# Weight loads one step ahead, separate buffers for step-size rows, and three feed-forward pairs begun early, in a one-core hybrid decoder layer

## The chip, the cores and the metric

The kernel runs on one core of one Trainium2 chip. The metric is device time in microseconds (us) of one launch. Three runs of the kernel before took 2627.57, 2632.49 and 2633.17 us; their median is 2632.49 us.

Engine names follow the profile: PE is TensorE's matrix multiply and PEld its weight load, DVE is VectorE, ACT is ScalarE, POOL is GpSimd, SP is SyncE, which in this kernel only issues transfers. "SPq" and "ACTq" in a row are an engine's instructions that issue transfers.

## The reference

One layer of a decoder that mixes three branches, for a prompt of 1024 tokens and a sample group of 8 tokens that use the same weights. Width D is 1024. Everything is in float32.

```
xn     = rmsnorm(x)
sc_B, sc_C, sc_x, z, xBC, dt, q, gates = split(xn @ w_in)
y_a    = (sc_B * conv3(sc_C * sc_x)) @ w_sc_out
xs,B,C = silu(conv4(xBC) + bias)                       # 32 heads x 64, 4 groups, state 128
dt     = softplus(dt + dt_bias);  a = -exp(a_log)
y_b    = group_rmsnorm((SSD(xs, dt, a, B, C) + d * xs) * silu(z)) @ w_ssm_out
k, v   = rmsnorm(mem) @ w_mem_k, rmsnorm(mem) @ w_mem_v   # 256 memory tokens
y_c    = softmax(q k^T / 16) v @ w_attn_o              # 4 heads x 256
x      = x + (sum of sigmoid(gates) * y_{a,b,c}) @ w_merge_o
x      = x + (silu(rmsnorm(x) @ w_gate) * (rmsnorm(x) @ w_up)) @ w_down
y      = rmsnorm(x)
```

The SSD of the prompt is computed in chunks of 128 tokens; the sample tokens take one step of the recurrence from given states. The memory keys and values, the convolution tails and the final states are outputs too. The feed-forward width is 2816.

## The kernel before, in words

**Layout.** Activations lie with the channel on the partitions and the tokens along the row: 1024 prompt columns and 8 sample columns, 1032 in all, so a block of 128 channels is one 128 x 1032 tile. A weight block is 1024 x 128: `wblock` gives it as eight slices of 128 x 128 in one 128 x 1024 tile. Every product of float32 numbers is done as three products of rounded halves: a value is split into `hi` (a copy on ACT into the reduced type) and `lo` (the difference, on DVE), and hi·hi, hi·lo and lo·hi are summed in PSUM.

**Helpers.** `weights` loads a block (raw, issued on SP), then splits it. Raw, hi and lo tiles have three buffers each, and `in_turn` keeps each of the three kinds in program order. `gemm` multiplies one block with all eight activation tiles and calls `tick` at `pace` places on the way. `tick` runs the next entry of the queue `pend`: so pieces of other work are laid between the matmuls of a stage. An entry None skips a place. `flush` runs the rest.

`strassen` does two weight blocks (256 output channels) with seven half products instead of eight, each 24 matmuls of 258 columns over four slices of 128 channels. The activations come as prepared forms: B11 and B21 are quarters, T1, nT2, T3 and T4 sums and differences of quarters, B22 the last quarter. The weights go with them as the block itself (A), as sums of blocks (S, T; made on DVE from the raw tiles) and as one half of a block (D). The partial results are put together from PSUM into three output parts o11, o12, o22; the fourth stays in PSUM (`pa`) for the caller. The products use PSUM tiles m0, m1, m2.

**Buffers.** Most transient tiles come from one pool `ev` with five buffers of 128 x 1036 floats (`ev_tile`), handed out in program order: a tile asked for later in the program gets a buffer only when an earlier one has been released by its last reader. From the merge on there is a pool `big` with eight buffers, and each holds a tile of the residual x2 at first.

**Order.** The program order of each engine is laid out when the kernel is built: a planner takes the calls in order and may move instructions of one engine past one another by its own estimate of costs, as far as their dependences allow. At run time each engine, and each engine's queue of transfers, works strictly in that order. SP issues nearly all loads, among them raw weights, `r<-ac_d` of the SSD stage and `gt`, `mg` of the output products, and many stores.

**Stages** (us of the profiled execution):
- to about 84: the norm of x, its transposes and splits, the small step-size product.
- 84 to 121: the first C block, z0 and z1 with `gemm`. Beside them, as ticks, run `dt_softplus`, `dt_sums`, `dt_rows` (two rows tiles acT and eaT of 32 x 1024) and `dt_sample` (four tiles exs of 8 x 1024, each transposed in eight parts into `ps_ex`). After them `mem_load` asks for the two memory tiles and computes their squares on ACT (L1006, into `junkm`) and their reciprocal roots.
- 121 to about 270: five pairs of z blocks (`z_pair`, Z2 to Z10) with four `mem_t` and sixteen `kv_block` entries as ticks, which compute the memory keys and values.
- then the xBC pairs (`xbc_pair`), with Z12 and Z14 among them.
- about 550 to 1330: the SSD in 32 chunk steps (four groups of eight chunks). The queue `pend` holds the pieces of the chunks; the main thread of products between them are the steps of `fillers` (three for each of eight short-convolution blocks, eight for q) and `gates` (24).
- to about 1785: attention and the sample states as pieces, between the output products `out_in` and `out_part` (L1350 to L1360: gate rows, weights `wo{i}{m}`, product `po`, sum `mg` through DRAM); then the last output product.
- to 1880: the merge (L1455). Two halves of 516 columns, eight output blocks each. The sum of squares is gathered while the blocks are made. `norm_half` (L1405 to L1418) turns the sum into `rf`, 1/rms in all 128 partitions: one matmul with a matrix of ones for each 258 columns, then a chain of six operations, five on DVE and one square root on ACT. The forms B11 and B21 of the first half are made during the second half of the merge, as ticks.
- 1880 to 2355: the feed-forward. First the remaining forms, L1490 to L1504, in the order T1 (with the normed quarter b12, `normed`, L1422), B22 (normed), nT2 and T3, T4; T1, nT2, T3 and T4 overwrite parts of x2 on the way. Then eleven gate pairs and eleven up pairs in turn, `hidden_pair`, each a `strassen` with outputs in `big` tiles; g0 is the first. Each pair of pairs is multiplied and stored to `h_d`.
- to the end: the down product and the final norm.

In `strassen` the product B21 comes after nT2, but for the first pair of a stage (`first`), where it comes directly after B11.

## Time and profile before

| what | value |
|---|---|
| runs shown | 2627.57, 2632.49, 2633.17 us |
| profiled execution, its own time | 2626.43 us |
| its span in the profile | 2624.5 us |
| mean granted TensorE clock | 0.978 of full |
| instructions | 42664 |
| TensorE busy | 2527.5 us |
| DVE busy | 1468.6 us |
| ACT busy | 933.1 us |
| POOL busy | 182.1 us |

The times in a profile are us from the start of the span. A row of the timeline has the start, the duration, the engine, the line of the kernel, the operation, the tile written and those read, the shapes, and in brackets how long the engine had been idle before and what released it. A row of the waits says which instruction of an engine waited for which other one, the sum of these waits, their count and the longest. A group row has the busy time and the mean of one in ns, and the idle time ahead. A row of windows has the busy time and, in brackets, the instructions of each engine in a stretch, then the mean granted clock of TensorE, the busy share of the DMA engines, and GB/s. Rows of transfers are named by the tile they fill.

### The profile page before, as it was taken

Reading aid. Unit: us, or ns where it says so; the run is one execution under the profiler, and the core shown is the slowest. Engines: PE = TensorE matmul, PEld = TensorE weight load, DVE = VectorE, ACT = ScalarE, POOL = GpSimd, SP = SyncE. Lnnn points to the kernel's source line nnn. Section 1 sums busy time; section 2 is a strip of 40 time slices with the busy share of each in tenths; the row PEclk is TensorE's granted clock in tenths of the full one; section 3 lists DMA queues with packets and bytes.
Section 4 is the critical chain, followed back from the end, with each engine's and each line's share of the span. In section 5 each row is a group of like instructions: output and inputs, shape, how many; then the busy total and the mean of one; then the engine's idle time right before and its main releaser. Section 6 shows DMA issues by size and latency. Waiting matters only on the chain.

```text
span 2624.5 us, 42664 instructions
## 1 busy us (share of the span) xinstructions
PE 2527.5 (96%) x18009; PEld 2458.8 (94%) x18009; DVE 1468.6 (56%) x2049; ACT 933.1 (36%) x1426; POOL 182.1 (7%) x203
## 2 busy tenths in 40 slices
PE   7899999999998999999999999999889999999998
PEld 6899999999998999999999997999889999999998
DVE  5744677866666655545576643344865454554316
ACT  5543444553333235254342321213343333342202
POOL 0000000013213123023000000000000000000000
PEclk8899999999999999999999999999989999999999
DMA  5244333376645556665487757844322222255211
GB/s 188 85 138 153 122 113 106 122 197 148 173 142 137 160 186 159 187 190 160 128 287 246 275 190 251 286 137 142 104 65 76 71 89 74 81 200 164 72 41 65
DMA packets 388301, 387.72 MB, mean 148 GB/s; under 512 B 15574, under 2 KB 334662, under 8 KB 388103
## 3 DMA queue, kind: packets, MB, share of 16 engines
q1 hardware_dynamic: 369534, 334.17, 42.3%
q10 hardware_dynamic: 18577, 50.84, 5.1%
q8 instruction: 141, 2.31, 0.4%
q14 instruction: 49, 0.40, 0.1%
HBM read 278.84 MB, written 106.34 MB: 147 GB/s over the span
## 4 chain that ended last, share of the span: by engine, by line
PE 70%; DMA 4%; DVE 4%; ACT 1%; issue 1%; SPq 0%; POOL 0%; ACTq 0%; DVEq 0%; POOLq 0%
PE po L167 10%; PE ps_g L167 10%; PE pd L167 8%; PE ps_scc L167 4%; PE pm L1455 4%; PE ps_scx L167 4%; PE ps_q L167 3%; PE ps_scb L167 3%; DMA kc<-in_cache_mem_k_dram 2%; PE py L730 1%; PE pss L748 1%; PE po L722 1%; PE u0m L218 1%; PE u20m L218 1%; PE g20m L218 1%; PE u18m L218 1%
## 5 line engine op out<-in xcount | busy, mean ns | idle before, releaser
L1568 DVE TENSOR_TENSOR x<-pd,x 128x1032 f32<-128x1032 f32 x24 | 29.6, 1231 | 130.8 <-PE pd L167 130.8
L675 ACT ACTIVATE r<-r,acum 128x128 f32<-128x128 f32 x256 | 78.9, 391 | 34.1 <-DMA r<-ac_d 32.7
L1355 DVE TENSOR_TENSOR gt<-po,gt 128x1032 f32<-128x1032 f32 x24 | 29.5, 1229 | 81.3 <-PE po L167 81.2
L709 POOL TENSOR_TENSOR xdd<-xdt,decst 128x512 f32<-128x512 f32 x32 | 46.5, 1455 | 272.0 <-DVE xdt L705 272.0
L534 DVE SCALAR_TENSOR_TENSOR ax<-u,prm,ax 128x1024 f32<-128x1024 f32 x44 | 56.3, 1280 | 0.0
L815 POOL TENSOR_TENSOR st<-st,xb 128x512 f32<-128x512 f32 x32 | 43.7, 1367 | 36.2 <-DVE xb L809 34.0
L702 ACT COPY bT<-bp 128x128 f32<-128x128 f32 x32 | 8.5, 265 | 105.3 <-DVE cbm L700 105.3
L739 DVE SCALAR_TENSOR_TENSOR x<-x,dpar,yt 128x128 f32<-128x128 f32 x128 | 37.5, 354 | 10.1 <-ACT yt L737 9.2
L703 DVE TENSOR_TENSOR r<-r,cbm 128x1024 f32<-128x1024 f32 x32 | 39.1, 1222 | 6.5 <-ACT r L676 5.9
L761 POOL TENSOR_TENSOR s<-s,cdec 128x512 f32<-128x512 f32 x28 | 39.1, 1396 | 44.9 <-DVE s L754 34.1
L748 PE MATMUL pss<-xdd,bT 128*128 128x512 f32 x64 | 33.7, 609 | 7.4 <-ACT bT L702 7.4
L754 DVE TENSOR_TENSOR s<-pss,s 128x512 f32<-128x512 f32 x28 | 19.2, 687 | 38.2 <-PE pss L748 38.2
L812 POOL TENSOR_TENSOR st<-st,es 128x512 f32<-128x512 f32 x32 | 36.5, 1142 | 18.7 <-DMA st<-in_state_ssm_dram 15.2
L730 PE MATMUL py<-r,xdt 128*64 128x128 f32 x512 | 35.0, 279 | 0.0
L700 DVE TENSOR_TENSOR cbm<-bp,tri 128x128 f32<-128x128 f32 x32 | 9.3, 290 | 45.7 <-PE bp L695 45.7
L676 ACT ACTIVATE r<-r 128x1024 f32<-128x1024 f32 x32 | 33.9, 1059 | 0.7
L726 DVE TENSOR_TENSOR yt<-po,ea 128x512 f32<-128x512 f32 x28 | 19.2, 686 | 25.9 <-PE po L722 25.9
L1391 DVE TENSOR_TENSOR gt<-po,gt 128x1032 f32<-128x1032 f32 x8 | 9.9, 1233 | 40.6 <-PE po L167 40.6
L1194 ACT ACTIVATE pr<-psa,mx 128x256 f32<-128x256 f32 x32 | 15.0, 472 | 48.3 <-DVE mx L1192 40.9
L1184 DVE TENSOR_TENSOR kc<-kc,qb 128x1024 f32<-128x1024 f32 x16 | 19.6, 1222 | 21.8 <-DMA kc<-in_cache_mem_k_dram 21.8
L730 PEld LDWEIGHTS py<-r,xdt 128*64 128x64 f32 x512 | 27.3, 136 | 4.2 <-issue 0.9
L821 DVE TENSOR_TENSOR xc<-bcb,st 128x512 f32<-128x512 f32 x32 | 21.9, 684 | 16.5 <-POOL st L815 15.1
(7946 smaller groups left out, 8666.9 us busy)
## 6 DMA issues: line engine op xcount, KB each, us to landing
gt<-gt_d SPq DMA_DIRECT2D x32, 516.0 KB
r<-ac_d SPq DMA_DIRECT2D x32, 512.0 KB
gt_d<-g ACTq DMA_DIRECT2D x24, 516.0 KB
mg_d<-gt SPq DMA_DIRECT2D x24, 516.0 KB
mg<-mg_d SPq DMA_DIRECT2D x24, 516.0 KB
xs_d<-ax ACTq DMA_DIRECT2D x22, 516.0 KB
hr<-h_d SPq DMA_DIRECT2D x22, 516.0 KB
zs_d<-z ACTq DMA_DIRECT2D x16, 516.0 KB
```

What stands on the lines that cost most here:

```text
L167: PE.matmul(ps[:, n, :CW], wt[:, ks], x[:, n * CW : (n + 1) * CW], start=(k == 0 and i == 0), stop=(k == nk - 1 and i == 2),)
L218: PE.matmul(ps[:, n, :HC], wt[:, ks], x[:, n * HC : (n + 1) * HC], start=(start and kt == 0 and i == 0), stop=(kt == 3 and i == 2), skip_g ...
L534: V.scalar_tensor_tensor(acc[:, :T], u[:, j : j + T], w[j], acc[:, :T], op0=ALU.mult, op1=ALU.add)
L675: S.activation(r[:, h, :], r[:, h, :], AF.Relu, scale=-1.0, bias=acum[:, c, h0 + h : h0 + h + 1])
L703: V.tensor_tensor(r, r, bc(cbm.unsqueeze(1), [P, HPG, P]), op=ALU.mult)
L709: G.tensor_tensor(b3(xdd, HPG), b3(xdt, HPG), bc(decst[:, c, hs].unsqueeze(2), [P, HPG, 64]), op=ALU.mult)
L730: PE.matmul(py[hp : hp + 64, (h // 2) * P : (h // 2 + 1) * P], xdt[:, h * 64 : (h + 1) * 64], r[:, h, :], start=True, stop=True,)
L739: V.scalar_tensor_tensor(xg[t][:, cs], xg[t][:, cs], dpar[:, g * 4 + t : g * 4 + t + 1], yt[:, t, :], op0=ALU.mult, op1=ALU.add,)
L748: PE.matmul(pss, bT, xdd, start=True, stop=True)
L761: ins = G.tensor_tensor(b3(s_new, HPG), b3(state["s"], HPG), bc(cdec[:, c, hs].unsqueeze(2), [P, HPG, 64]), op=ALU.mult,)
L815: G.tensor_tensor(st, st, xb, op=ALU.add)
L1455: PE.matmul(ps[:, n, :HC], wt[:, ks], x[:, half * HT + n * HC : half * HT + (n + 1) * HC], start=(k == 0 and i == 0), stop=(k == KD - 1 an ...
```

## The change

Six things are changed.

1. A step of the SSD stage and of the output products is now a `Step` that knows its weights. `run_next` issues the raw load of the following step's weights before it runs the current step; `weights` takes the loaded tile if there is one.
2. acT, eaT and the four exs tiles come from the pool of the step-size stage, under one tag with two buffers, no longer from `ev`. The squares of the memory tiles and their roots move from `mem_load` into an entry `mem_rms` of `pend`, behind a None; the squares are written into a tile that is filled later (`memT`), so `junkm` goes.
3. Z12 moves from between the xBC pairs to behind Z10, ahead of the `flush`. The flag `first` goes: for Z2 the product B21 stands at its usual place.
4. `norm_half` is called once for a half: six matmuls, each with 128 columns of the squares as weights, give the sums of the 516 tokens as six columns (three pieces that overlap for each 258), the chain runs on these columns, and six transposes and two ACT copies spread the result over the partitions.
5. `st_early` does the products B11 and B21 of the first gate pair, the first up pair and the second gate pair (g0, u0, g2) ahead of the remaining forms, and holds their sums in three ev tiles. It loads the first raw block of each pair for that, once more than before. These three pairs then run `strassen` with five products; three more operations on DVE and one copy on ACT put the parts together, in four output parts.
6. The remaining forms come in the order T1, nT2 (which now does the normed quarter b22), T3, B22, T4. For T3 both the difference and `lo` are on GpSimd. The weight sums of g0 stand between the forms: S after T1 (`st_sums`), T after T3 (`st_sums2`).

```diff
...
-    def weights(src, name):
+    loaded = {}
+
+    def load_raw(src, name):
         raw = wp.tile([P, 1024], F32, tag="raw", name=name + "r")
...
+        return raw
+
+    class Step:
+
+
+        def __init__(self, src, name, run):
+            self.src, self.name, self.run = src, name, run
+
+        def __call__(self):
+            self.run()
+
+    def run_next(*queues):
+
+        q = [f for d in queues for f in d]
+        (queues[0] or queues[-1]).popleft()
+        if len(q) > 1 and isinstance(q[1], Step):
+            loaded[q[1].name] = load_raw(q[1].src, q[1].name)
+        q[0]()
+
+    def weights(src, name):
+        raw = loaded.pop(name, None)
+        if raw is None:
+            raw = load_raw(src, name)
         hi = wp.tile([P, 1024], F32R, tag="whi", name=name + "h")
         lo = wp.tile([P, 1024], F32R, tag="wlo", name=name + "l")
         in_turn("hi", S.copy(hi, raw))
...
+    def st_prod(forms, ps, w, off, f, start):
+        for kt in range(4):
+            xh, xl = forms[f][kt]
+            ks = slice(off + kt * P, off + (kt + 1) * P)
+            for i, (wt, x) in enumerate(((w[0], xh), (w[0], xl), (w[1], xh))):
+                for n in range(2):
+                    PE.matmul(
+                        ps[:, n, :HC], wt[:, ks], x[:, n * HC : (n + 1) * HC],
+                        start=(start and kt == 0 and i == 0), stop=(kt == 3 and i == 2),
+                        skip_group_check=True,
+                    )
+
+    def st_early(blocks, forms):
+
+
+        held = []
+        for i, (src1, nm, o1) in enumerate(blocks):
+            wA = st_split(st_raw(src1, f"{nm}Er"), f"{nm}E")
+            ps = st_ps(f"m{i}", f"{nm}e")
+            st_prod(forms, ps, wA, 0, "B11", True)
+            S.copy(h3(o1[:, HS[1]]), hv(ps))
+            held.append((wA, ps, o1))
+        for wA, ps, o1 in held:
+            st_prod(forms, ps, wA, 512, "B21", False)
+            S.copy(h3(o1[:, HS[0]]), hv(ps))
+
+    def st_sums(src1, src2, nm, sums):
         raw1, raw2 = st_raw(src1, f"{nm}r1"), st_raw(src2, f"{nm}r2")
...
+        sa = sums(f"{nm}sa")
+        V.tensor_add(sa[:, :512], raw2[:, :512], raw2[:, 512:])
+        V.tensor_add(sa[:, 512:], sa[:, :512], raw1[:, :512])
+        return raw1, raw2, sa, st_split(sa, f"{nm}S")
+
+    def st_sums2(raw1, raw2, sa, nm, sums):
+        sb = sums(f"{nm}sb")
+        V.tensor_add(sb[:, :512], raw1[:, :512], raw2[:, :512])
+        V.scalar_tensor_tensor(
+            sb[:, 512:], sa[:, 512:], -1.0, raw1[:, 512:], op0=ALU.mult, op1=ALU.subtract
+        )
+        return st_split(sb, f"{nm}T")
+
+    def strassen(src1, src2, forms, nm, sums, outs, early=None, after_t3=None, ready=None):
+
+
+        if ready is None and early is None:
+            raw1, raw2 = st_raw(src1, f"{nm}r1"), st_raw(src2, f"{nm}r2")
         tags = ("m0", "m1", "m2") if count[0] % 2 == 0 else ("m2", "m1", "m0")
         count[0] += 1
-        pa, pb, pc = (pst[0].tile([P, 2, 512], F32, tag=t, name=f"{nm}{t}") for t in tags)
+        pa, pb = (st_ps(t, f"{nm}{t}") for t in tags[:2])
 
         def prod(ps, w, off, f, start):
...
+        o11, o12, o21, o22 = outs()
+        if early is None:
+            pc = st_ps(tags[2], f"{nm}{tags[2]}")
+            wA = st_split(raw1, f"{nm}A")
+            prod(pa, wA, 0, "B11", True)
+            S.copy(h3(o11), hv(pa))
+        tick()
+        if ready is not None:
+            raw1, raw2, sa, wS, wT = ready
+        elif early is not None:
+            raw1, raw2, sa, wS = st_sums(src1, src2, nm, sums)
+        else:
+            sa = sums(f"{nm}sa")
+            V.tensor_add(sa[:, :512], raw2[:, :512], raw2[:, 512:])
+            V.tensor_add(sa[:, 512:], sa[:, :512], raw1[:, :512])
+            wS = st_split(sa, f"{nm}S")
+        prod(pb, wS, 0, "T1", True)
+        S.copy(h3(o22), hv(pb))
+        prod(pa, wS, 512, "nT2", early is not None)
+        if early is None:
+            S.copy(h3(o12), hv(pa))
             prod(pc, wA, 512, "B21", True)
             V.tensor_tensor(h3(o11), hv(pc), h3(o11), op=ALU.add)
-
-        wA = st_split(raw1, f"{nm}A")
-        prod(pa, wA, 0, "B11", True)
-        S.copy(h3(o11), hv(pa))
+        else:
+            S.copy(o21, o12)
+            V.tensor_sub(o22, o22, o12)
+            V.tensor_tensor(h3(o12), hv(pa), h3(o12), op=ALU.add)
...
+        if ready is None:
+            wT = st_sums2(raw1, raw2, sa, nm, sums)
         prod(pa, wT, 0, "T3", False)
         if after_t3 is not None:
             after_t3()
...
     def dt_rows():
-        act_ = ev_tile("acT", (HEADS, T))
-        eat_ = ev_tile("eaT", (HEADS, T))
+        act_, eat_ = (pd_.tile([HEADS, T], F32, tag="wide", bufs=2, name=n) for n in ("acT", "eaT"))
...
         for i in range(4):
-            exs = ev_tile(f"exs{i}", (NS, 1024))
+            exs = pd_.tile([NS, 1024], F32, tag="wide", bufs=2, name=f"exs{i}")
...
         def s0():
             hold["c"] = c_()
 
+        def at(col, nm, f):
+            return Step(wblock(w_in, col + ct * P), f"w{nm}{ct}", f)
+
...
-        return [s0, s1, s2]
+        return [at(C_SCC, "scc", s0), at(C_SCX, "scx", s1), at(C_SCB, "scb", s2)]
 
...
             t = ev_tile(f"mem{m}", (P, D))
             SY.dma_start(t, a["mem_prompt"][0, m * P : (m + 1) * P, :])
             mem_sb.append(t)
-        junk = ev_tile("junkm", (P, D))
+
+    def mem_rms():
         for m in range(2):
+            junk = memT[m][0].rearrange("p k c -> p (k c)")
             S.activation(junk, mem_sb[m], AF.Square, accum_out=mst[:, m : m + 1])
         rsqrt(pm, mrs, mst, D, [P, 2], "m")
 
...
     mem_load()
+    pend.extend([None, mem_rms])
     pend.extend(lambda m=m, half=half: mem_t(m, half) for m in range(2) for half in range(2))
     pend.extend(lambda j=j, q=q: kv_block(j, q) for j in range(8) for q in range(2))
     z_step(1)
...
-    for i in (2, 4, 6, 8, 10):
+    for i in (2, 4, 6, 8, 10, 12):
         z_pair(i)
     flush()
     mem_stack.close()
...
-    z_pair(12)
     xbc_pair(4, 5)
     xbc_pair(6, 7)
     xbc_pair(8, 9)
...
     while pend:
-        (fillers or gates).popleft()()
+        run_next(fillers, gates)
...
-                lambda w=w, m=m, i=i: out_part(w, m, (0, 8, 8)[i] + m, i > 0, f"{i}{m}") for m in range(KD)
+                Step(
+                    wblock(w, m * P), f"wo{i}{m}",
+                    lambda w=w, m=m, i=i: out_part(w, m, (0, 8, 8)[i] + m, i > 0, f"{i}{m}"),
+                )
+                for m in range(KD)
             )
         while pend:
-            gates.popleft()()
+            run_next(gates)
...
-    def norm_half(half, sq, i):
-        if i == 0:
-            rfs[half] = ev_tile(f"rf{half}")
+    def norm_half(half, sq):
+        rfs[half] = ev_tile(f"rf{half}")
         t = rfs[half]
...
+        starts = [n * HC + c for n in range(2) for c in (0, P, HC - P)]
+        ps = sm_ps(f"psf{half}")
+        for i, c in enumerate(starts):
+            PE.matmul(ps[:, i : i + 1], sq[:, c : c + P], ones[:, 0:1], start=True, stop=True)
+        r, v = t[:, 600:606], t[:, 606:612]
+        s_ = t[:, 612:618]
+        V.tensor_scalar(v, ps[:, :6], 1.0 / D, EPS, op0=ALU.mult, op1=ALU.add)
+        S.activation(s_, v, AF.Sqrt)
+        V.reciprocal(r, s_)
+        V.tensor_mul(s_, r, r)
+        V.scalar_tensor_tensor(s_, v, -0.5, s_, op0=ALU.mult, op1=ALU.mult)
+        V.scalar_tensor_tensor(r, s_, 1.5, r, op0=ALU.add, op1=ALU.mult)
+        for n in range(2):
+            ps = sm_ps(f"psr{half}{n}")
+            for i in range(3):
+                c = starts[i]
+                PE.transpose(ps[:, c : c + P], bc(r[:, 3 * n + i : 3 * n + i + 1], [P, P]), ident)
+            S.copy(t[:, n * HC : (n + 1) * HC], ps[:, :HC])
 
...
         if half == 0:
-            pend.extend([None, None] + [lambda i=i, sq=sq: norm_half(0, sq, i) for i in range(2)] + [None])
+            pend.extend([None, None] + [lambda sq=sq: norm_half(0, sq)] + [None])
             for kt in range(4):
                 pend.extend([lambda kt=kt: form_first(kt), None, lambda kt=kt: form_second(kt), None])
         else:
             flush()
-            for i in range(2):
-                norm_half(1, sq, i)
+            norm_half(1, sq)
...
+    ffn = {"g": a["w_ffn_gate"][0], "u": a["w_ffn_up"][0]}
+    early = {(nm, j): ev_tile(f"{nm}{j}e") for nm, j in (("g", 0), ("u", 0), ("g", 2))}
+    st_early([(wblock(ffn[nm], j * P), f"{nm}{j}", t[:, :TT]) for (nm, j), t in early.items()], forms)
     for kt in range(4):
         b12, b11 = normed(kt, 1), x2[kt][:, HS[0]]
         V.tensor_sub(b11, b12, b11)
         form("T1", kt, b11)
+    ev_sums = lambda n: ev_tile(n, (P, 1024))
+    g0 = st_sums(wblock(ffn["g"], 0), wblock(ffn["g"], P), "g0", ev_sums)
     for kt in range(4):
-        form("B22", kt, normed(kt + 4, 1))
-    for kt in range(4):
-        t1, b12, b22 = x2[kt][:, HS[0]], x2[kt][:, HS[1]], x2[kt + 4][:, HS[1]]
+        t1, b22 = x2[kt][:, HS[0]], normed(kt + 4, 1)
         V.tensor_sub(t1, t1, b22)
         form("nT2", kt, t1)
-        V.tensor_sub(b12, b22, b12)
-        form("T3", kt, b12)
+    for kt in range(4):
+        b12, b22 = x2[kt][:, HS[1]], x2[kt + 4][:, HS[1]]
+        G.tensor_tensor(b12, b22, b12, op=ALU.subtract)
+        form("T3", kt, b12, G)
+    g0 = (*g0, st_sums2(*g0[:3], "g0", ev_sums))
+    for kt in range(4):
+        form("B22", kt, x2[kt + 4][:, HS[1]])
     for kt in range(4):
         t2, b21 = x2[kt][:, HS[0]], x2[kt + 4][:, HS[0]]
         V.scalar_tensor_tensor(t2, t2, -1.0, b21, op0=ALU.mult, op1=ALU.subtract)
         form("T4", kt, t2)
 
...
+        e = early.get((nm, j))
 
         def outs():
-            o.extend([big(f"{nm}{j}o1"), big(f"{nm}{j}o2")])
-            return o[0][:, HS[0]], o[0][:, HS[1]], o[1][:, HS[1]]
-
+            o.extend([big(f"{nm}{j}o1") if e is None else e[:, :TT], big(f"{nm}{j}o2")])
+            return tuple(t[:, c] for t in o for c in HS)
+
+        src = ffn[nm]
         pa = strassen(
             wblock(src, j * P), wblock(src, (j + 1) * P), forms, f"{nm}{j}",
-            lambda n: ev_tile(n, (P, 1024)), outs, nm == "g" and j == 0,
+            ev_sums, outs, e, ready=g0 if (nm, j) == ("g", 0) else None,
         )
-        return o[0], o[1], pa
+        return o[0], o[1], pa if e is None else h3(pa)
 
...
     st_stack.close()
```

88 lines of the change are left out of this document (26 added, 62 removed).

## The prediction

> **What bounds the kernel now.** I read the page first. Its parts one and two have the span, the busy time of each engine, and TensorE's busy tenths in 40 slices of 65.6 us.
>
> ```profile
> span 2624.5 us, 42664 instructions
> PE 2527.5 (96%) x18009; PEld 2458.8 (94%) x18009; DVE 1468.6 (56%) x2049; ACT 933.1 (36%) x1426; POOL 182.1 (7%) x203
> PE   7899999999998999999999999999889999999998
> ```
>
> TensorE bounds it: 2624.5 − 2527.5 = 97 us idle in all, and no product is removed by this change. So a gain can only come from idle time, or from matmuls that run at a lowered clock behind idle time. The tenths dip in the first two slices, at 787 to 853 us and at 1837 to 1968 us. Next I read the waits of TensorE (who waited for whom, sum, count, longest).
>
> ```profile
> PE g0m L218 <- ACT g0o L232: 13.3, 1, 13.3
> PE po L167 <- ACT wo24h L127: 7.8, 1, 7.8
> PE g0m L218 <- ACT T10h L263: 7.5, 1, 7.5
> PE pss L748 <- ACT bT L702: 7.4, 1, 7.4
> PE Z2m L218 <- ACT z L621: 5.3, 1, 5.3
> PE Z4m L218 <- ACT Z4Th L198: 2.5, 1, 2.5
> PE Z8m L218 <- ACT Z8Th L198: 2.5, 1, 2.5
> ```
>
> Each is a single event. Then I cut windows around them; the columns are microseconds, busy PE, weight loads, DVE, ACT, POOL, the granted clock, the DMA share and GB/s.
>
> ```profile
> 95.90:116.00 20.10, 17.55 (x116) 15.91 (x114) 16.39 (x26) 11.85 (x17) 0.20 (x1) 0.92 0.17 52
> 116.00:121.30 5.30, 0.02 (x1) 0.00 (x0) 1.78 (x5) 2.07 (x4) 0.00 (x0) 0.60 0.94 316
> 121.30:141.00 19.70, 19.41 (x137) 19.01 (x138) 13.38 (x29) 12.20 (x25) 0.00 (x0) 0.85 0.34 118
> 1631.30:1643.70 12.40, 2.72 (x24) 0.88 (x22) 2.49 (x3) 2.37 (x6) 0.00 (x0) 0.69 0.80 295
> 1643.70:1657.80 14.10, 14.10 (x73) 14.10 (x74) 3.65 (x3) 2.39 (x3) 0.00 (x0) 0.79 0.83 226
> 1886.40:1893.90 7.50, 0.05 (x1) 0.00 (x0) 7.50 (x13) 2.53 (x5) 0.00 (x0) 0.64 0.16 46
> 1901.50:1914.80 13.30, 0.04 (x1) 0.00 (x0) 13.30 (x23) 7.28 (x12) 0.00 (x0) 0.53 0.00 0
> 1914.80:1920.80 6.00, 5.57 (x28) 5.36 (x28) 5.99 (x10) 3.42 (x6) 0.00 (x0) 0.63 0.00 0
> 1949.30:2354.70 405.40, 405.39 (x3362) 405.18 (x3360) 203.92 (x254) 137.32 (x178) 0.00 (x0) 1.00 0.29 94
> ```
>
> The reader is to see three places of different kinds: at 116–121 us TensorE waits with a full DMA, at 1631–1644 us it waits for weights, and at 1886–1920 us DVE is busy all the time, so the feed-forward forms bound the work there. From 1949 to 2355 us TensorE is never idle: 20 pairs, 140 half products of 24 matmuls, 405.4/140 = 2.896 us each.
>
> **Part one: the exs and acT/eaT rows in their own pool, the squares of mem as a tick, z12 moved.**
>
> ```profile
> 98.38 0.59 ACT L491 ACTIVATE eaT<-ps_acT 32x512 f32<-32x512 f32 x1 [0.24 <-DVE acT L490]
> 98.88 0.99 ACT L600 COPY uC<-ps_C 128x1032 f32<-128x1032 f32 x1
> 114.97 1.03 ACT L621 ACTIVATE z<-ps_z 128x1032 f32<-128x1032 f32 x1 [2.91 <-PE ps_ex L510]
> 119.21 1.06 ACT L1006 ACTIVATE junkm<-mem 128x1024 f32<-128x1024 f32 x1 [3.20 <-DMA mem<-in_mem_prompt_dram]
> 120.26 1.01 ACT L621 ACTIVATE z<-ps_z 128x1032 f32<-128x1032 f32 x1
> ```
>
> The five ev buffers are handed out in program order. So uC, z0 and the two mem tiles can't be written until the rows ahead of them (acT, eaT, the four exs) are done with: z0's Silu runs right behind the exs chain, the mem loads start only then, the Square of mem waits for them, and z1's Silu, which Z2's first matmul waits for, stands behind that Square on ACT. With the rows in a pool of their own and the Square pended, this chain goes. Idle in the first two windows is 2.55 + 5.28 = 7.8 us; the lowered clock costs 17.55 × 0.08 = 1.4 us and 19.41 × 0.15 = 2.9 us. That is 12.1 us in all. The exs chain itself stays, now through two buffers, and the Square still runs before mem's transposes; I leave 2 us for that: −10, bounds −12.5 and +4 (the wait for mem comes back inside Z2, with as much again at half clock; mem_t and all the key and value ticks queue behind it).
>
> Two new ticks shift the key and value blocks, and z12 now runs beside them. Z4 and Z8 lose 2.5 us each where ACT copies a key block ahead of the T weights; I count one more such place: +2.5, bounds 0 and +4. Z12's own products only move, and the xbc pair that it leaves has no wait in the list above.
>
> **Part two: weights asked for one step ahead.** Of each step the raw load on SP is issued before the previous step's pieces; the cast and the subtraction stay.
>
> ```profile
> 1001.95 0.37 SPq L122 DMA_DIRECT2D wg5r<-in_w_in_dram  x1
> 1044.94 1.05 ACT L127 CAST wg5h<-wg5r 128x1024 fp32r<-128x1024 f32 x1 [1.12 <-PE ps_g L167]
> 1637.64 0.69 SPq L122 DMA_DIRECT2D wo24r<-in_w_ssm_out_dram  x1
> 1642.60 1.04 ACT L127 CAST wo24h<-wo24r 128x1024 fp32r<-128x1024 f32 x1
> ```
>
> Elsewhere a load is asked 43 us before its cast (wg5), so earlier asking buys nothing there; at wo24 it is asked 5 us ahead, behind the stores of the last attention pieces on SP. This ask now stands ahead of them. The window 1631–1644 holds 12.40 − 2.72 = 9.7 us idle, of which 7.8 for this weight; the next one runs at 0.79, 14.10 × 0.21 = 3.0 us. The small gaps of 1.9 us stay and keep some of the low clock: I take −9 (7.8 and 1.2 of the 3.0), bounds 0 and −11.
>
> The Trainium skill (TensorE: Matmul & The Clock Gate, Part 1) says that the clock falls after an idle window of about 3.4 us. By that rule the gaps of 1.9 us would not lower it, all 3.0 us would return, and the sum below would be about 2 us lower.
>
> What an early ask can cost is another matter: SP works in order, and each ask waits at its head until one of the three raw buffers is free. Behind it stand, in the SSD stage, the loads of r.
>
> ```profile
> 835.60 0.66 SPq L669 DMA_DIRECT2D r<-ac_d  x1
> 835.60 12.51 DMA r<-ac_d
> r<-ac_d SPq DMA_DIRECT2D x32, 512.0 KB
> ```
>
> This load took 12.5 us and stands in the chain that ended last, ahead of the wait for bT of 7.4 us. It can come out better (−11 with its clock) or worse by the new order of instructions. I take 0.
>
> **Part three: the feed-forward start.** Now: B11, then the norm of the second half, T1, nT2, and so on, with DVE as the bound.
>
> ```profile
> 1879.59 0.48 PE L218 MATMUL g0m<-B110h,g0Ah 128*128 128x258 f32 x2 [0.88 <-DVE x L1462]
> 1881.74 0.43 DVE L1413 TENSOR_SCALAR rf<-psf 128x258 f32<-128x258 f32 x1 [0.85 <-PE psf L1412]
> 1890.27 0.42 DVE L1418 SCALAR_TENSOR_TENSOR rf<-sq,rf 128x258 f32<-128x258 f32 x1
> 1913.69 0.62 ACT L263 CAST T40h<-x 128x516 fp32r<-128x516 f32 x1 [0.65 <-DVE x L1502]
> 1914.21 0.58 ACT L232 COPY g0o<-g0m 128x516 f32<-128x516 f32 x1
> ```
>
> The 13.3 us wait is not one for ACT: g0's output needs a `big` buffer, and that is one of x2's, which is free only once the first T4 form has been written (1913.7). g0's last product ends at 1929.0, reckoned back from the end of the last pair over the 147 half products of the other 21: 2354.7 − 147 × 2.896.
>
> After the change six half products (B11 and B21 of g0, u0, g2) come first: 17.4 us of TensorE, to about 1898, with outputs in ev buffers. They cover the T1 and part of the nT2 forms. g0, u0, g2 then have five products each. But o21 and o22 are still `big` tiles and still wait for the first T4 form. So the date is set by DVE's list up to there. The norm chain took 1881.74 to 1890.69, 8.95 us for two halves; on six columns it must be under one half, 4.5, and I take 3: rf at about 1884.8. Six matmuls and six transposes for each half, against two matmuls: +1 in all, bounds 0 and +2. Then: T1 12 operations, nT2 12, B22 4, T4 2, at 7.50/13 = 13.30/23 = 0.58 us, 17.4; g0's sums, four of half width, 2.3; and the subtractions of S, T and one E, 1.2 each.
>
> ```profile
> 812.47 1.23 DVE L128 TENSOR_TENSOR wscc7l<-wscc7r,wscc7h 128x1024 fp32r<-128x1024 f32 x1 [1.56 <-ACT wscc7h L127]
> 831.37 2.07 DVE L128 TENSOR_TENSOR wscx7l<-wscx7r,wscx7h 128x1024 fp32r<-128x1024 f32 x1
> 832.43 2.16 POOL L815 TENSOR_TENSOR st<-st,xb 128x512 f32<-128x512 f32 x1
> L815 POOL TENSOR_TENSOR st<-st,xb 128x512 f32<-128x512 f32 x32 | 43.7, 1367 | 36.2 <-DVE xb L809 34.0
> ```
>
> The first of these rows gives the 1.2. In sum 17.4 + 2.3 + 3.6 = 23.3, to 1908.1. The T3 forms move to POOL: eight operations of 1.37 us, 11 us. They aren't free, since the same subtraction took 1.23 us alone and 2.07 beside POOL work, which itself took 2.16 for 1.37: DVE lost 0.84 in 2.07 us that hold about 2.07 × 1.37/2.16 = 1.3 us of POOL work, between 0 and all of it. I take three quarters, towards the upper end, since T3 falls into the stretch in which DVE is never idle: +8.4, to 1916.5 (bounds 1908.1 and 1919.1). Behind that stand the copy of o22, two DVE operations, 3 × 0.58 = 1.7, then the products T3, B22 and T4, 8.7, and half clock at their start (28 matmuls in 5.57 us is 0.2 us each, against 0.121: 1.9 us for one product). g0 ends at 1916.5 + 12.3 = 1928.8. 143 products stay behind it instead of 147: gain 1929.0 + 4 × 2.896 − 1928.8 = 11.8, less 2 for waits that the early pairs meet (three extra E splits, 512 KB each to load, during merge): −10, bounds −18 (no contention) and −2.
>
> The Trainium skill (SBUF — State Buffer, Who interferes with whom) says that a DVE instruction with two SBUF inputs and a GpSimd instruction that reads SBUF share a port pair under an exclusive lock, the loser blocked for the whole instruction. By that rule all 11 us fall on DVE, and the gain here is about 7. The rows agree in kind: both engines lengthen.
>
> **Sum.** −10 + 2.5 − 9 − 10 + 1 = −25.5 on the profiled execution's 2626.43 us (span 2624.5 and 1.93 around it): 2600.9. The runs shown lie 1.1 to 6.7 us above that execution, the median 6.06; with 4 for that, 2605 us.
>
> **The rivals.** Two gains can fail alone. The ask at wo24 stays behind the stores, if the order of SP puts it there: 2605 + 9 = 2614. Or POOL locks DVE for the whole of T3, and T3's own forms, at 2.16 us each, 17.3 us, come later than the nT2 product: then the feed-forward start gains 2, not 10, and the time is 2613. For it speaks the DVE's full windows; against it, that TensorE has six products to do meanwhile. Larger: the wait for bT goes by chance (−11) or POOL costs DVE nothing (−8): about 2587 to 2597.
>
> Slower: early asks at the head of SP hold back the loads of r. Against it, the wait list holds just one such stall in 32 chunks, and asks are few (one a step); for it, a stall there already cost 7.4 us with a landing of 12.5. If each chunk waits 1 us more, 32 us come on top: 2637. It decides from 30.5/32, about 0.95 us in each chunk; the place to see it is r's idle time on ACT.
>
> No change: the same mechanism at about 0.8 us a chunk, which uses up the gain. About 0.2% (5.3 us) is what a measurement of this kernel can tell.
>
> **How the numbers follow.** Likeliest 0.52 (own range 2597 to 2612); one or both of the two gains failing 0.22; larger 0.10; no measurable change 0.04; slower 0.12. That gives faster 0.84, same 0.04, slower 0.12. The range runs from the larger case, 2585, to where both gains fail and part one gives little, 2628: it leaves out the slower case and the ends of the larger one.
>
> **What would show it.** Right: z1's Silu no longer behind a Square, Z2's first matmul at about 111 us; no wait of po for wo24h; the waits for g0o and T10h gone or under 5 us; g0's end minus the four products at about 1929. A third wait of 2.5 us at a Z pair. Wrong: r's waits on ACT longer in many chunks; a wait of g0m for T3 forms; DVE operations of 516 columns well over 0.75 us beside POOL; a new wait at Z2 for mem.

## The result and the profile after

The changed kernel took 2607.4 us (median of four runs, 2603.75 to 2610.7) where the kernel before took 2631.22 us on the same chip: ratio 0.9911, 95% interval 0.9893 to 0.9929. The forecast was 2605 us, faster.

The head of the page of the changed kernel:

```profile
span 2601.7 us, 42760 instructions
PE 2521.7 (97%) x18037; PEld 2453.8 (94%) x18037; DVE 1466.5 (56%) x2037; ACT 936.6 (36%) x1434; POOL 197.9 (8%) x211
```

TensorE's idle time fell from 97 to 80 us (2601.7 − 2521.7). Its busy time fell as well, by 5.8 us with 28 matmuls more, so this part is time at a lowered clock. Its waits after, the longest ones of the places concerned:

```profile
PE pss L815 <- ACT bT L769: 6.5, 1, 6.5
PE g0m L236 <- DVE nT22l L329: 4.3, 2, 3.6
PE g0m L236 <- DVE g0e L309: 3.7, 1, 3.7
PE Z4m L236 <- ACT Z4Th L223: 2.5, 1, 2.5
PE Z8m L236 <- ACT Z8Th L223: 2.5, 1, 2.5
PE Z12m L236 <- ACT Z12Th L223: 2.5, 1, 2.5
```

The waits for wo24h and T10h are gone, the one for g0o is down to 0.8 us, the wait for bT stands about as it was, and a third Z pair waits 2.5 us. Smaller waits for forms, and one for an addition (g0e), have come up at g0 in place of the two long ones.

To see where the time went, I cut both executions at the same six instructions: the first z0 product, the first product of the SSD stage, the first product with wo00, the first with wo24, the first of the feed-forward, the first of the down product. Windows of the kernel before, and then of the changed one (columns as in the prediction):

```profile
84.14:547.77 463.63, 446.80 (x3621) 442.87 (x3619) 301.09 (x419) 213.75 (x280) 6.88 (x46) 0.98 0.40 126
547.77:1334.14 786.37, 773.49 (x5148) 742.18 (x5148) 466.25 (x668) 302.59 (x512) 173.83 (x147) 0.99 0.60 167
1334.14:1643.69 309.55, 294.13 (x1904) 277.76 (x1904) 165.09 (x225) 87.72 (x171) 0.00 (x0) 0.98 0.71 245
1879.59:2355.57 475.98, 452.23 (x3700) 450.30 (x3701) 260.84 (x339) 166.81 (x220) 0.00 (x0) 0.97 0.27 87
```

```profile
79.39:540.50 461.11, 446.47 (x3620) 442.17 (x3618) 302.58 (x423) 217.26 (x283) 6.94 (x46) 0.99 0.39 127
540.50:1329.26 788.76, 772.37 (x5147) 740.79 (x5147) 465.61 (x666) 302.36 (x512) 173.98 (x147) 0.99 0.61 167
1329.26:1628.48 299.22, 291.65 (x1885) 277.14 (x1886) 163.74 (x223) 86.38 (x166) 0.00 (x0) 0.99 0.71 241
1864.84:2332.49 467.65, 454.74 (x3714) 452.76 (x3715) 261.99 (x331) 165.39 (x223) 15.65 (x8) 0.98 0.28 90
```

| stretch | before | after | difference | forecast |
|---|---|---|---|---|
| start to z0 | 84.1 | 79.4 | −4.7 | 0 |
| z and xBC pairs | 463.6 | 461.1 | −2.5 | −7.5 |
| SSD stage | 786.4 | 788.8 | +2.4 | 0 |
| wo00 to wo24 | 309.6 | 299.2 | −10.3 | −9 |
| wo24 to the feed-forward | 235.9 | 236.4 | +0.5 | 0 |
| feed-forward | 476.0 | 467.7 | −8.3 | −9 |
| down product and end | 268.9 | 269.2 | +0.3 | 0 |
| span | 2624.5 | 2601.7 | −22.8 | −25.5 |

The sum is near, but two of its terms are not: the start gained 4.7 us with no part of the change in it, and the z stage gained a third of what was forecast.

### The profile page after: what moved, and what is told of

Same layout as the page of the kernel before. It is cut to its first block, busy times and chain, and to the rows that moved or that the text cites. A ratio compares the mean times of both kernels' runs of the same rounds, so it can differ in the third digit from the quotient of the medians.

```text
span 2601.7 us, 42760 instructions
## 1 busy us (share of the span) xinstructions
PE 2521.7 (97%) x18037; PEld 2453.8 (94%) x18037; DVE 1466.5 (56%) x2037; ACT 936.6 (36%) x1434; POOL 197.9 (8%) x211
## 4 chain that ended last, share of the span: by engine, by line
PE 68%; DMA 5%; DVE 4%; issue 1%; ACT 1%; SPq 0%; POOL 0%; ACTq 0%; DVEq 0%; POOLq 0%
PE ps_g L192 10%; PE po L192 10%; PE pd L192 8%; PE ps_scc L192 4%; PE pm L1535 4%; PE ps_q L192 4%; PE ps_scx L192 3%; PE ps_scb L192 3%; DMA kc<-in_cache_mem_k_dram 1%; PE py L797 1%; PE pss L815 1%; PE po L789 1%; DMA r<-ac_d 1%; PE u20m L236 1%; PE g20m L236 1%
## 5 line engine op out<-in xcount | busy, mean ns | idle before, releaser
L742 ACT ACTIVATE r<-r,acum 128x128 f32<-128x128 f32 x256 | 78.9, 391 | 36.2 <-DMA r<-ac_d 34.8
L1424 DVE TENSOR_TENSOR gt<-po,gt 128x1032 f32<-128x1032 f32 x24 | 29.5, 1230 | 70.4 <-PE po L192 69.1
L1583 POOL TENSOR_TENSOR x<-x,x 128x516 f32<-128x516 f32 x4 | 8.9, 2235 | 635.8 <-DVE x L1502 635.8
L1542 DVE TENSOR_TENSOR x<-pm,xT 128x516 f32<-128x516 f32 x16 | 11.1, 695 | 36.2 <-PE pm L1535 36.2
```

The source lines that it names most:

```text
L742: S.activation(r[:, h, :], r[:, h, :], AF.Relu, scale=-1.0, bias=acum[:, c, h0 + h : h0 + h + 1])
```

## The experiments

Times below are compared with runs of the kernel before on the same chip, or by stretches of the profile. A stretch is that of one profiled execution. How far one order spreads can be read from the versions whose edit lies elsewhere: with the changed order the z and xBC stretch took 460.7 to 461.1 us in five executions, and the feed-forward 466.9 to 467.7 us in six; the profile above is the longest of each. In the SSD stage TensorE has the same order of instructions in all versions, and it took 784.9 to 790.2 us. Six versions ran once, five of them in 2602 to 2607 us and the one without asks in the output products in 2615; single whole times can't tell 2 or 3 us apart, so for these versions only the stretches are read.

**T3 on DVE.** Both operations of T3 go back to DVE:

```diff
-        G.tensor_tensor(b12, b22, b12, op=ALU.subtract)
-        form("T3", kt, b12, G)
+        V.tensor_sub(b12, b22, b12)
+        form("T3", kt, b12)
```

> The changed kernel with the T3 forms (difference and lo) back on DVE. Theory 1, POOL and DVE exclude each other: in the changed kernel nine DVE operations of 516 columns beside POOL took about 1.77 us each against a pitch of 0.60, 10.5 us lost, to save DVE eight operations of 0.60, 4.8 us. Then DVE's list to the first T4 form gets 5.7 us shorter, no 516-column operation of DVE is above 0.76 us, and the time falls by 3 to 7 us against the changed kernel, to about 2602. Theory 2, POOL's help pays and the late nT2 lo is only a matter of order: DVE gets eight more operations, the time rises by up to 5 us, to about 2612.

It took 2596.87 us against 2627.18 (ratio 0.9888, interval 0.9871 to 0.9904). First rows of POOL (the second is a group) and of DVE in the changed kernel, with its window of that time; then the window of equal length of this run, its feed-forward stretch, and its longest wait at g0.

```profile
1879.99 3.90 POOL L1583 TENSOR_TENSOR x<-x,x 128x516 f32<-128x516 f32 x1 [633.76 <-DVE x L1502]
L329 POOL TENSOR_TENSOR T30l<-x,T30h 128x516 fp32r<-128x516 f32 x2 | 3.4, 1736 | 0.0
1882.04 0.69 DVE L329 TENSOR_TENSOR nT20l<-x,nT20h 128x516 fp32r<-128x516 f32 x1
1882.64 2.46 DVE L1502 SCALAR_TENSOR_TENSOR x<-x,prm,rf 128x516 f32<-128x516 f32 x2
1891.44 1.77 DVE L1579 TENSOR_TENSOR x<-x,x 128x516 f32<-128x516 f32 x1
1898.18 0.68 DVE L1590 SCALAR_TENSOR_TENSOR x<-x,x 128x516 f32<-128x516 f32 x1
1882.60:1898.20 15.60, 8.25 (x60) 7.33 (x58) 15.60 (x13) 6.51 (x12) 13.04 (x8) 0.84 0.02 5
```

```profile
1884.80:1900.40 15.60, 7.75 (x64) 7.47 (x62) 15.60 (x26) 8.18 (x14) 0.00 (x0) 0.87 0.12 34
1867.02:2329.50 462.48, 451.35 (x3714) 450.53 (x3715) 258.22 (x339) 165.10 (x223) 0.00 (x0) 0.99 0.28 90
PE g0m L236 <- ACT g0o L300: 9.5, 1, 9.5
```

In 15.6 us DVE and POOL together have 13 + 8 operations, counting those that the edges of the window cut; DVE alone has 26. An operation of 516 columns that takes 0.69 alone takes 1.77 beside POOL, and POOL's take some 1.7 (its first one, ahead of the window, 3.90). The rows read as if the two engines took turns here, one operation each. The feed-forward is 5.2 us shorter with T3 on DVE (4.4 against the shortest with the changed order), where theory 1 had 3 to 7. Of the 5.2 us, 1.8 are idle time of TensorE, and 3.4 are its busy time for the same products (454.74 and 451.35), so the larger part is time at a lowered clock behind the waits. The 9.5 us wait for the buffer of x2 is then the one that shows; the smaller waits for forms are gone.

**One early pair instead of three.**

```diff
-    early = {... for nm, j in (("g", 0), ("u", 0), ("g", 2))}
+    early = {... for nm, j in (("g", 0),)}
```

> The changed kernel with early products for g0 alone, two half products instead of six. Theory 1, DVE's list of forms sets the end of g0: g0 ends as long after its first early product as now (53 us), and four half products of 2.896 us more stand behind it: plus 11.6 us on the feed-forward stage, less up to 1.5 us for two E splits that DVE is spared. Theory 2, TensorE sets the end of g0 and the early products are only moved: the stage stays within 2 us.

```profile
1861.73:2336.06 474.33, 457.18 (x3715) 454.11 (x3715) 260.65 (x328) 166.59 (x222) 14.55 (x8) 0.97 0.27 88
```

6.7 us longer, between the theories: four products later by 11.6 us would be theory 1, so by this sum g0 itself ends 4.9 us earlier. Two E splits of 1.2 us that DVE is spared are 2.4 of it; the other 2.5 I can't assign. TensorE's columns show 4.2 of the 6.7 us as idle time and 2.4 as busy time for the same products. The extra early products are worth some 7 us, not 11.6.

**The norm's chain on 258 columns.**

```diff
-        for i, c in enumerate(starts):
-            PE.matmul(ps[:, i : i + 1], sq[:, c : c + P], ones[:, 0:1], start=True, stop=True)
...
+        for i in range(2):
+            c = slice(i * HC, (i + 1) * HC)
+            ps = sm_ps(f"psf{half}{i}")
+            PE.matmul(ps[:, :HC], ones, sq[:, c], start=True, stop=True)
...
```

> The changed kernel with the norm's chain on 258 columns, as before the change. Theory 1, DVE's list sets the end of g0: the chain takes about 9 us again instead of 4.0 (from the last square sum to the first normed quarter), and the feed-forward stage gets 3 to 6 us longer. Theory 2, the early products cover it: the stage stays within 1 us.

Two rows of DVE of this run, the chain's first operation and the first normed quarter, and its feed-forward window; the last row is the first normed quarter in the changed kernel:

```profile
1866.76 0.86 DVE L1486 TENSOR_SCALAR rf<-psf 128x258 f32<-128x258 f32 x2 [0.79 <-PE psf L1485]
1873.05 1.42 DVE L1495 SCALAR_TENSOR_TENSOR x<-x,prm,rf 128x516 f32<-128x516 f32 x2
1864.09:2333.40 469.31, 454.35 (x3700) 451.53 (x3701) 267.50 (x336) 165.86 (x222) 13.27 (x8) 0.98 0.28 90
```

```profile
1870.90 1.42 DVE L1502 SCALAR_TENSOR_TENSOR x<-x,prm,rf 128x516 f32<-128x516 f32 x2 [1.37 <-ACT rf L1498]
```

The stage is 1.7 us longer (2.4 against the shortest with the changed order), less than theory 1 had and more than theory 2. Counted from the first feed-forward product, the first normed quarter comes at 8.96 us with the wide chain (1873.05 − 1864.09) and at 6.06 with the narrow one (1870.90 − 1864.84): from where the wide chain starts, 2.67 us after that product, it takes 6.3 us, and in its place the short chain with its matmuls, transposes and copies takes 3.4.

**The second tick behind T3.** A version that goes beyond the change: in `strassen`

```diff
-        tick()
         if ready is None:
             wT = st_sums2(raw1, raw2, sa, nm, sums)
         prod(pa, wT, 0, "T3", False)
+        tick()
```

> The changed kernel with the second tick of a pair moved behind the T3 product, so that the T weights are cast on ACT ahead of a key or value block's copies. Theory 1, the three waits of 2.5 us at Z4, Z8 and Z12 come only from ACT's order: all three go, the time falls by 5 to 8 us against the changed kernel, to about 2600. Theory 2, the wait only changes its place (the block's own weights must now be split between two half products 2.9 us apart): new waits of 1 to 3 us in most pairs, time the same or up to 8 us longer.

It took 2591.08 us (ratio 0.9871, interval 0.9853 to 0.9888), and all three waits are gone. The stretch of the z and xBC pairs:

```profile
79.81:529.57 449.76, 442.43 (x3621) 439.23 (x3619) 301.80 (x421) 216.72 (x283) 7.46 (x46) 1.00 0.40 130
```

11.4 us shorter: 7.5 for the waits, and 4.0 less busy time of TensorE for the same products (446.47 to 442.43), since some of the waits had lowered its clock behind them. More than theory 1 expected.

**Both edits.** 

> Both edits at once: second tick behind the T3 product, T3 forms on DVE. They lie in different stages, so theory 1 adds them: minus 11.4 us (first z product to the first product of the SSD stage, 461.1 to 449.8) and minus 5.2 us (feed-forward stage, 467.7 to 462.5) against the changed kernel; ratio to the kernel before about 0.985, some 2587 us on this chip. Theory 2, part of the gain of the tick run was its SSD stage (2.3 us shorter, by another order): then 2 to 3 us less is gained.

2584.75 us against 2625.54: ratio 0.984, interval 0.9826 to 0.9855, the best version here, faster than both kernels (the changed one has 0.9911 against the kernel before on its own chip).

```profile
1851.05:2313.68 462.63, 451.50 (x3715) 450.68 (x3715) 258.44 (x339) 165.22 (x224) 0.00 (x0) 0.99 0.28 91
80.58:530.39 449.81, 442.61 (x3621) 439.32 (x3619) 301.75 (x420) 216.61 (x283) 7.42 (x46) 1.00 0.40 130
```

The two gains add to within 0.2 us in their stretches.

**The first T4 form earlier.** As the former run, and in the order of the forms:

```diff
+    form_t4(0)
     g0 = (*g0, st_sums2(*g0[:3], "g0", ev_sums))
     for kt in range(4):
         form("B22", kt, x2[kt + 4][:, HS[1]])
-    for kt in range(4):
+    for kt in range(1, 4):
+        form_t4(kt)
```

> As the former, and the first T4 form ahead of g0's second weight sums and of B22. Theory 1, what g0 waits for (9.5 us ahead of its B22 product with T3 on DVE) is the buffer of x2 that the first T4 form releases: the wait falls by 4 to 6 us and the feed-forward stage by 2 to 4 us against the former run. Theory 2, another wait takes its place at once (the addition into g0's early part, which DVE does behind all T4 forms, holds back T3): the stage stays within 1 us.

```profile
1852.07:2315.97 463.90, 453.02 (x3714) 451.73 (x3715) 258.23 (x339) 165.29 (x223) 0.00 (x0) 0.99 0.28 91
PE g0m L236 <- ACT g0Th L223: 6.8, 1, 6.8
```

Nothing gained (2586.06 us, the stretch 1.3 us longer): the wait for the buffer is gone, which shows that it was the first T4 form that it waited for, and a wait for g0's T weights takes its place, whose sums DVE now makes later. So DVE's list as a whole looks like the bound there, not one place in it.

**Weights asked ahead in the output products alone**, in the kernel before: `run_next`, `Step` and `loaded` as in the change, used for the `out_part` steps only.

> The kernel before with one part alone: weights asked one step ahead in the output products. Theory 1, the wait of 7.8 us for wo24's weights goes by this part alone: from the first wo00 matmul to the first wo24 matmul 299 to 301 us instead of 309.6, the whole 9 to 11 us shorter. Theory 2, without the other parts the request still comes behind the stores on SP: a wait of more than 4 us stays. At the start, where this kernel has the order of the kernel before: if the 4.7 us that the changed kernel gained ahead of the first z product are chance of the clock, that product starts anywhere from 79 to 84 us; if they are the order's, at 84.

2612.04 against 2625.54 us (ratio 0.9941, interval 0.9926 to 0.9956). The wait for wo24h is gone; the stretch from wo00 to wo24:

```profile
1332.07:1630.52 298.45, 292.30 (x1885) 278.01 (x1885) 163.81 (x223) 86.32 (x166) 0.00 (x0) 0.98 0.69 242
```

11.1 us shorter than in the kernel before. This run also bears on the start. Up to the attention stage every engine has the instructions of the kernel before in the same order, and still its first z0 product starts at 79.03 us, not at 84.14. A window of 4 us of the kernel before; then, of this run, z0's first product, the same window, and the SSD stage:

```profile
52.00:56.00 4.00, 4.00 (x15) 3.17 (x16) 3.44 (x9) 2.64 (x7) 0.00 (x0) 0.52 0.22 76
```

```profile
79.03 0.48 PE L192 MATMUL ps_z<-xnh,wz0h 128*128 128x344 f32 x2
52.00:56.00 4.00, 4.00 (x24) 3.38 (x25) 3.46 (x9) 2.38 (x8) 0.00 (x0) 1.00 0.22 77
541.92:1332.07 790.15, 772.91 (x5147) 741.40 (x5148) 465.82 (x668) 302.65 (x512) 175.74 (x147) 0.99 0.60 167
```

The clock was granted at half in this window in one execution, and in full in the other. In the eleven profiles of the other versions z0 starts at 78.6 to 81.4 us. So the 4.7 us of the profiled difference are no gain of the change, but chance of that one execution, or at most of the chip that it ran on. The last row says the same of the SSD stage: 790.2 us with the instruction order that took 786.4, so the +2.4 us there is within what one order shows.

**Squares at the load.**

```diff
-    pend.extend([None, mem_rms])
+    mem_rms()
```

> The changed kernel with the squares of the memory tiles computed where they are loaded, not as a tick. Theory 1, the Square stands on ACT ahead of z1's Silu and waits for the memory tiles: Z2 starts 2 to 5 us later than 26.6 us after the first z product. Theory 2, with the rows out of ev the tiles come early enough, and the tick buys nothing: Z2 starts within 1 us of that; the key and value ticks then come one or two places earlier, and the number of 2.5 us waits at the Z pairs can change.

```profile
107.34 0.39 PE L236 MATMUL Z2m<-xnh,Z2Ah 128*128 128x258 f32 x1 [2.06 <-ACT z L688]
80.69:542.26 461.57, 446.62 (x3620) 442.20 (x3618) 301.25 (x419) 217.26 (x283) 6.90 (x46) 0.99 0.39 126
```

Z2 starts 26.65 us after z0's first product (107.34 − 80.69), and the stretch has 461.6 us against 461.1: the tick for the squares buys nothing, theory 2. This was run with the rows out of ev only; with the rows in ev the squares at the load are not tested.

**The rows back in ev.**

```diff
-        act_, eat_ = (pd_.tile([HEADS, T], F32, tag="wide", bufs=2, name=n) for n in ("acT", "eaT"))
+        act_, eat_ = (ev_tile(n, (HEADS, T)) for n in ("acT", "eaT"))
...
-            exs = pd_.tile([NS, 1024], F32, tag="wide", bufs=2, name=f"exs{i}")
+            exs = ev_tile(f"exs{i}", (NS, 1024))
```

> The changed kernel with acT, eaT and the four exs tiles in ev again; the squares stay a tick. Theory 1, these tiles hold the buffers that uC, z0 and the memory tiles wait for: Z2 starts 32 to 38 us after the first z product instead of 26.6, with a wait for z's Silu of 2 to 6 us ahead of it. Up to the first product of the SSD stage 3 to 6 us are lost. Theory 2, the squares as a tick were the part that counted: Z2 starts within 1 us of 26.6.

```profile
113.80 0.58 PE L236 MATMUL Z2m<-xnh,Z2Ah 128*128 128x258 f32 x1 [1.42 <-ACT z L688]
80.62:544.86 464.24, 448.72 (x3621) 444.26 (x3619) 302.65 (x419) 213.81 (x280) 6.86 (x46) 0.98 0.39 126
```

Z2 starts 33.2 us after z0 (113.80 − 80.62) instead of 26.6, as theory 1 had it, but the whole stretch is only 3.1 us longer. The wait ahead of it was smaller (1.4 us) than theory 1 expected. The exs transposes start 27.1 us after z0 in this run, ahead of Z2, and 28.6 us after it in the changed kernel, inside Z2. The first key block comes at 63.1 us here and at 59.7 in the changed kernel; so about half of what Z2's start gains is used up by work that then runs within Z2.

**Z12 back.**

```diff
-    for i in (2, 4, 6, 8, 10, 12):
+    for i in (2, 4, 6, 8, 10):
...
     xbc_pair(2, 3)
+    z_pair(12)
```

> The changed kernel with Z12 at its old place among the xBC pairs. Theory 1, Z12 beside the key and value ticks only adds a third wait: that wait goes, and with the half clock behind it the stretch from the first z product to the first product of the SSD stage is 3 to 4 us shorter than 461.1. Theory 2, the ticks that Z12 would have covered now run bare ahead of the xBC pairs, their weights late: the stretch is the same or up to 8 us longer.

```profile
81.36:540.11 458.75, 446.53 (x3621) 442.27 (x3619) 302.02 (x420) 217.06 (x283) 6.88 (x46) 0.99 0.40 128
```

2.4 us shorter than 461.1, and clear of the 460.7 to 461.1 that the changed order shows: the move of Z12 cost its one wait. That is a little under the 3 to 4 us of theory 1. TensorE's busy time is the same (446.5), so over the stretch no lowered clock went with the wait.

**Weights asked ahead in the SSD stage only**: the `out_part` steps are plain calls again.

> The changed kernel with the weights asked ahead in the SSD stage only, not in the output products. Theory 1, the request ahead of the output products is all that the asks bring: the wait for wo24's weights of about 8 us is back, the stretch from the first wo00 to the first wo24 matmul is 309 to 310 us, and the SSD stage stays between 786 and 790 us as in the other runs. Theory 2, the other changes have moved the stores on SP as well: the wait is under 4 us.

```profile
PE po L192 <- ACT wo24h L152: 9.3, 1, 9.3
1325.26:1638.59 313.33, 294.82 (x1904) 277.80 (x1904) 165.18 (x225) 87.78 (x171) 0.00 (x0) 0.98 0.70 244
```

The wait is back, and the stretch is 14.1 us longer than in the changed kernel, 3 us above what theory 1 had. The SSD stage took 785.6 us, within the spread; the early ask has no effect there that one could see.

## Why the prediction was right, and where it was not

**Direction and size.** The forecast of 2605 us lies 2.4 us off the median. Two of the three gains, the weights and the feed-forward start, came from where the prediction put them and within 1.3 us of their size. The third was mis-sized by 5 to 7 us; in the profiled pair of executions, 4.7 us at the start that the change didn't bring stood in for most of that. That the profiled sum came so near is in part luck.

**Weights one step ahead.** Right: forecast −9, measured −10.3 in the changed kernel and −11.1 with this part alone, up to the first wo24 product. That cut is not quite fair: with the early ask some 20 matmuls of the attention pieces come behind this product instead of ahead of it (1904 against 1885). Up to the feed-forward, where the work is the same, it is 545.5 us before, 535.6 in the changed kernel and 533.2 with this part alone: −9.9 and −12.2. The low clock behind the wait went too, where the prediction left most of it standing (last row below: 1.00 where it was 0.79). The estimate of 2 us more by the clock rule of the Trainium skill (TensorE: Matmul & The Clock Gate, Part 1) fits no worse than the forecast, but this is no test of the rule: it was about the small gaps of 1.9 us, and they went as well, since TensorE is busy all the time from 1616.5 to 1643 us. The request now reaches SP at 1618.9 us, ahead of the last stores, and the cast follows 6.6 us later:

```profile
1618.93 0.42 SPq L124 DMA_DIRECT2D wo24r<-in_w_ssm_out_dram  x1
1625.50 1.05 ACT L152 CAST wo24h<-wo24r 128x1024 fp32r<-128x1024 f32 x1 [1.31 <-DMA wo24r<-in_w_ssm_out_dram]
1629.00:1643.00 14.00, 14.00 (x98) 12.51 (x97) 4.77 (x4) 2.01 (x5) 0.00 (x0) 1.00 0.82 262
```

**Rows out of ev, squares, Z12.** The step that failed is "12.1 us in all ... I leave 2 us for that: −10". The mechanism was right: with the rows in ev, Z2 starts 6.6 us later, and the sign that the prediction named for it came true (Z2's first matmul comes 26.6 us after z0's, which counted from z0 in the kernel before is 110.8 us; forecast 111). But over the stretch the pool is worth 3.1 us and the tick for the squares nothing; the rest of the difference to the kernel before, 1 to 2 us, is not assigned. The term took Z2's start for the end of the stretch. Rows of the changed kernel (Z2's first product, the first exs transposes, the first key block), then the first key block of the kernel before:

```profile
106.03 0.38 PE L236 MATMUL Z2m<-xnh,Z2Ah 128*128 128x258 f32 x1 [2.08 <-ACT z L688]
108.03 0.47 PE L574 MATMUL ps_ex<-ident,exs 8*128 8x8 f32 x5
139.08 0.28 PE L1109 MATMUL ps_kv<-wkv00h,memh 128*128 128x256 f32 x1
```

```profile
141.95 0.28 PE L1040 MATMUL ps_kv<-wkv00h,memh 128*128 128x256 f32 x1
```

The exs transposes now run inside Z2 instead of ahead of it, and the first key block comes 59.7 us after z0's first product (139.08 − 79.39) where it came 57.8 after it (141.95 − 84.14). The last key or value block runs at 294 us, behind Z12, where it ran at 280 us, behind Z10. So part of Z2's earlier start is paid back in Z2 and behind Z12. The lowered clock, charged with 4.3 us of the 12.1, brought next to nothing: TensorE's busy time in the stretch is 446.8 us before and 446.5 after. Z12's price, forecast +2.5, was +2.4.

**The feed-forward start.** Forecast −10 and +1, measured −8.3 (−9.1 with the shortest of the other executions), with errors that cancel. The contention term had the right size: 8.4 us forecast (three quarters of 11 would be 8.2). From 1882.64 to 1898.18 us DVE did eleven operations in 15.5 us; at 0.60 each that is 6.6, so 8.9 were lost. What the prediction did not draw from its own terms is that the 8.4 us buy only the eight operations of T3, 8 × 0.58 = 4.6 us: by them the move to POOL loses 3.8. The first T4 form came at 35.0 us after the first product, forecast 36.9 (1916.5 − 1879.6):

```profile
1899.19 0.62 ACT L328 CAST T40h<-x 128x516 fp32r<-128x516 f32 x1
1898.30:1908.50 10.20, 5.72 (x28) 5.21 (x28) 10.20 (x17) 5.42 (x10) 0.00 (x0) 0.67 0.14 42
1908.50:1914.00 5.50, 5.46 (x27) 5.46 (x28) 3.05 (x6) 3.60 (x4) 0.00 (x0) 0.54 0.54 156
```

(1899.19 + 0.62 − 1864.84). What was too short is the tail of 12.3 us behind it. The 143 half products of the others, 414.1 us, leave 467.7 − 414.1 = 53.5 us for g0's end, 18.5 behind the T4 form. T1 and nT2 were multiplied by then, as forecast, though only just: TensorE had waited 3.6 us for the last `lo` of nT2. But behind the T4 form it waited 3.7 us more for the addition into g0's early part, which stands behind all T4 forms on DVE; the prediction has no such wait. And the products B22 and T3, on both sides of that wait, ran largely at a lowered clock (the last two rows above: 55 matmuls in 11.2 us busy, 4.5 more than at 0.121 each), where the forecast had 1.9 us for one product. On the other side, the 2 us for waits of the early pairs didn't come (0.9 us). The term for the norm, 3 instead of 8.95, counted on 6 us; the first normed quarter came 2.9 us earlier than with the wide chain in the same place, and that is worth 1.7 us.

The Trainium skill's rule (SBUF — State Buffer, Who interferes with whom), one instruction waiting for the whole of the other, is in line with the rows in kind: 1.77 us is the operation's own 0.69 and about 1.1 more. In price DVE lost 8.9 us, between the 8.4 of the sum and the 11 that the prediction worked out by the rule.

**The rivals.** No run shows asks holding back the loads of r: ACT's idle time for r, where the prediction wanted to see it, is 34.8 us in six waits after and 32.7 in six before, and the wait for bT stayed at 6.5 us. The sign of being wrong that did come is DVE operations well over 0.75 us beside POOL. The gain of the early products hides it: the move of T3 to POOL is the part of the change that loses, by 4.4 to 5.2 us.

## What to carry to other kernels

An early start of one instruction is not a gain of its stretch: ask which work has only moved behind it, and compare stretches that end where all of that work is done. Where an engine is never idle, handing work with two inputs in SBUF from VectorE to GpSimd is worth checking against a count of both engines' operations in equal time, since here the pair did less than VectorE alone. A wait of one buffer, one order or one late request can be found by name in the wait list, and its worth is the wait and, where the clock fell, the clock behind it.

## What the runs showed of the hardware

The same wait of 2.5 us had different prices. Windows of the changed kernel right behind the waits at Z4 and at Z8:

```profile
155.90:158.00 2.10, 2.07 (x9) 2.07 (x10) 2.09 (x2) 1.45 (x2) 0.00 (x0) 0.50 0.69 240
217.80:220.00 2.20, 2.17 (x18) 2.17 (x19) 2.19 (x2) 1.45 (x2) 0.00 (x0) 1.00 0.75 259
```

Behind Z4 the granted clock is 0.50 and 9 matmuls run in 2.1 us, behind Z8 it is 1.00 and 18 run in 2.2. Behind Z12 it is 0.57. The Trainium skill (TensorE: Matmul & The Clock Gate, Part 1) says that the window which decides is free-running and 3.4 us long; that a wait of 2.5 us, shorter than the window, lowers the clock at some places and not at others is in line with a window that runs on regardless, though not with a need for a whole idle window. One profiled execution can carry some 5 us that another with the same order of instructions doesn't, as the start of the kernel before did.
